# The attention output product on float16 parts for 24 of its 32 steps, and a new count of filler units around the heads

## The chip, the cores and the metric

The kernel runs on one core of a Trainium2 chip, in one launch. The metric is the device time of that core in microseconds. Before the change three runs took 1767.74, 1769.35 and 1769.62 us; their median, 1769.35 us, is the time before. The kernel's output must be the reference's in float32.

## The reference

A transformer of two layers with 256 tokens, 256 context tokens and 2048 model features, in float32. Layer 0 mixes by a Fourier transform, layer 1 by attention with 64 query heads and 8 key/value heads of 64 features, with a window, a context and a sink. Both end in an output product from 4096 branch features back to 2048. What bears on this case, cut:

```python
def _attend_with_sink(q, k, v, sink, mask=None):
    s = jnp.einsum('bqhgd,bkhd->bhgqk', q, k).astype(jnp.float32) * (ATTN_HEAD_DIM ** -0.5)
    ...
    p = jax.nn.softmax(jnp.concatenate([s, sk], axis=-1), axis=-1)[..., :-1]
    return jnp.einsum('bhgqk,bkhd->bqhgd', p.astype(v.dtype), v)

# _attention_branch
    y = jnp.moveaxis(o, 0, 1).reshape(b, n, D_BRANCH) * jax.nn.silu(z)

# reference, for each layer i
        h = _rmsnorm(x, norm_g[i]) * (1 + scale) + shift
        ...
        x = x + gate * (y @ w_out[i])
    return _rmsnorm(x, final_g)
```

With 256 tokens and 4096 branch features, y @ w_out[1] is a product of 256 x 4096 by 4096 x 2048: 32 steps of 128 branch features ("k" below), two blocks of 128 tokens ("tb") and four blocks of 512 columns.

## The kernel before, in words

**Numbers in two parts.** A float32 product is made of three matmuls on a high and a low part of each operand: high by high, high by low, low by high (`mm3`, lines 145 to 147). There are two kinds of parts. Float32r parts come from `split` (lines 66 and 67): ScalarE casts the high part, VectorE (in some places GpSimd) subtracts it for the low part. Float16 parts come from `split16` (lines 137 and 138): ScalarE writes the value times a power of two as float16, VectorE writes the rest; the power of two keeps the values in float16's range, and is found from a sum of squares of the whole operand. Before the change layer 0's products, the K/V product of layer 1 and the softmax weights use float16 parts; layer 1's q and z products and its output product use float32r parts.

**The stages around the change.**
- The Fourier output product (weights wo0, until about 1000 us) runs on float16 parts. Beside it, loads on GpSimd's queue bring tiles of 128 x 512 of the next weights (wkv), and ScalarE squares and sums them (line 827) for their scale.
- The K/V product: 8 weight groups (kg) of two steps each, one weight half of 128 x 1024 for each step, eight PSUM banks as its output. Then the evacuation (lines 1197 and 1198) and the making of v.
- Attention: 64 heads in a loop of 66 passes. Pass i has the scores of head i (lines 1422 and 1423), the softmax (1424 to 1430), the weights as float16 parts f (1439 on ScalarE, 1440 on VectorE), their transposition into ft, and the value product of head i − 2 (1457 and 1458). For heads 0 to 61 the transposition is a DMA on SP's queue (1442), for heads 62 and 63 sixteen transposes of TensorE (1449) and two copies (1450).
- Filler units. While one head's softmax runs, TensorE does pieces of other products: `filler()` is called twice in each pass and emits one unit. A unit is a piece of a q or z product (lines 1386 and 1388 and the lines of `mm3`), or two steps of the output product's first 512 columns (weights wo1a, `o1_step`, twelve matmuls). There are 64 units of q, 64 of z and 12 of the output product, 140; ten come ahead of the first head. 130 remain for 132 calls, so the last pass has none.
- The output product's rest: the remaining four double steps of wo1a, then wo1b (16 groups of two steps, columns 512 to 1535, 12 matmuls a step) and wo1c (8 groups of four steps, the last 512 columns, 6 matmuls a step), all on float32r parts. y's parts are made by `y_split`: steps 0 to 15 in a ring of tiles named ys, 16 to 23 in tiles of the pool act, 24 to 31 in another ring named ys.
- The end: gate, residual (x2), final norm, store.

**What sets the order.** Each engine works through its own row of instructions in order, and waits on semaphores. The row is set when the program is built, by a scheduler that follows the order of the code and its own model of times; `tc.issue_after(x)` keeps an instruction behind x. DMAs wait in their queue's row in the same way: SP's row carries the weight loads ("raw") and the DMA transposes, GpSimd's the tiles that are only squared and some others. Tiles come from rings with a fixed number of buffers: a load into a ring waits for the tile that was in its buffer before.

## Time and profile before

| | |
|---|---|
| median of three runs | 1769.35 us (1767.74 to 1769.62) |
| profiled execution, whole time | 1769.55 us |
| its span on the core | 1767.8 us |
| mean granted TensorE clock | 0.997 |
| Fourier output product | until about 1000 us |
| K/V product, TensorE | 1002.4 to 1085 us |
| attention, first scores to last value product | about 1127 to 1609 us |
| rest of the output product | about 1609 to 1759 us |
| norm and store after the last matmul | about 9 us |

The profile is of one execution. A row of a timeline has the start of a group, its time, the engine, the line, the operation, output and inputs, the count, and in brackets the idle time ahead of it with what ended it. Matmuls overlap in the array, so the duration of one is longer than the distance to the next; how long it holds TensorE is seen from one start to the next. A float32r matmul is shown as f32. A table of windows gives the busy time of each engine in each stretch, the granted clock, the busy share of the DMA engines and the rate that they moved.

### The profile page before, as it was taken

What the parts mean: (1) busy time and instruction counts of PE and PEld (TensorE: products, weight loads), DVE (VectorE), ACT (ScalarE), POOL (GpSimd) and SP (SyncE); (2) the same over time, 40 slices, a digit from 0 to 9 for tenths busy, and PEclk for the clock granted to TensorE, in tenths of its full rate; (3) what the DMA queues carried; (4) which work ended last, traced back from release to release, by engine and by line L of the source; (5) the groups of instructions that cost most, each with busy time, mean ns of one, the idle gap of its engine ahead of it and who ended that gap; (6) DMA issues with size and microseconds to landing.
All of it is one profiled execution on the core that took longest, in us unless ns stands there. A gap on an engine that the chain in (4) does not pass through costs nothing. (4 is left out here: it accounts for less than half of the span.)

```text
span 1767.8 us, 26608 instructions
## 1 busy us (share of the span) xinstructions
PE 1732.2 (98%) x9517; PEld 1187.7 (67%) x9517; DVE 1406.6 (80%) x2454; ACT 1090.5 (62%) x2069; POOL 331.9 (19%) x440
## 2 busy tenths in 40 slices
PE   6999999999999999999999999999999999999997
PEld 4679999644444444446444746788888888887886
DVE  5779889797677786877797695899999989997455
ACT  5545556477777755465223554687888878895343
POOL 0002111212222214212101001302312230233010
PEclk9999999999999999999999999999999999999999
DMA  9998998778998969977996432588988898887543
GB/s 394 417 356 247 279 278 254 289 286 314 332 305 312 312 228 371 368 267 259 341 316 212 142 137 74 169 215 199 223 207 206 213 215 206 207 212 258 190 167 143
DMA packets 229077, 447.29 MB, mean 253 GB/s; under 512 B 155888, under 2 KB 156288, under 8 KB 202064
## 3 DMA queue, kind: packets, MB, share of 16 engines
q1 hardware_dynamic: 182784, 331.93, 58.3%
q0 software_dynamic: 42016, 106.70, 19.4%
q10 hardware_dynamic: 4144, 6.95, 1.2%
q8 instruction: 75, 1.23, 0.3%
q14 instruction: 58, 0.48, 0.1%
HBM read 400.43 MB, written 12.59 MB: 234 GB/s over the span
## 5 line engine op out<-in xcount | busy, mean ns | idle before, releaser
L67 DVE TENSOR_TENSOR wl<-raw,wh 128x1024 fp32r<-128x1024 f32 x197 | 262.5, 1338 | 108.0 <-ACT wh L66 80.3
L66 ACT CAST wh<-raw 128x1024 fp32r<-128x1024 f32 x197 | 205.5, 1044 | 138.1 <-PE ps L146 97.0
L146 PE MATMUL ps<-act,wf 128*128 128x512 f16 x512 | 194.0, 379 | 0.0
L147 PE MATMUL ps<-act,wf 128*128 128x512 f16 x512 | 191.1, 379 | 0.0
L145 PE MATMUL ps<-act,wf 128*128 128x512 f16 x512 | 189.8, 379 | 0.6 <-ACT wf L137 0.2
L1386 PE MATMUL ps<-h,wh 128*128 128x512 f32 x512 | 185.0, 397 | 0.0
L145 PE MATMUL ps<-y,wf 128*128 128x512 f16 x448 | 169.8, 379 | 0.8 <-ACT wf L137 0.8
L147 PEld LDWEIGHTS <-wf 128*128 128x128 f16 x960 | 93.8, 98 | 114.0 <-DVE wf L138 0.9
L146 PE MATMUL ps<-y,wf 128*128 128x512 f16 x448 | 169.8, 379 | 0.0
L145 PEld LDWEIGHTS <-wf 128*128 128x128 f16 x960 | 93.7, 98 | 113.3 <-ACT wf L137 4.2
L147 PE MATMUL ps<-y,wf 128*128 128x512 f16 x448 | 167.4, 379 | 0.4 <-DVE wf L138 0.4
L146 PEld LDWEIGHTS <-wf 128*128 128x128 f16 x960 | 93.9, 98 | 109.0
L137 ACT ACTIVATE wf<-raw,nrm 128x1024 f16<-128x1024 f32 x56 | 63.4, 1145 | 137.1 <-DVE acc L792 68.5
L1388 PE MATMUL ps<-h,wl 128*128 128x256 f32 x512 | 138.6, 281 | 0.0
L138 DVE SCALAR_TENSOR_TENSOR wf<-raw,tn,wf 128x1024 f16<-128x1024 f32 x64 | 79.8, 1281 | 42.0 <-ACT wf L137 41.9
L1440 DVE SCALAR_TENSOR_TENSOR f<-p,sm,f 128x512 f16<-128x512 f32 x128 | 105.8, 847 | 9.0 <-ACT f L1439 8.7
L790 POOL DMA_DIRECT2D wa<-in_adw x64 | 34.0, 532 | 403.2 <-PE ps L147 149.7
L1427 ACT ACTIVATE p<-ps,mx 128x512 f32<-128x512 f32 x128 | 87.9, 689 | 35.0 <-DVE mx L1424 29.6
L1439 ACT ACTIVATE f<-p,sm 128x512 f16<-128x512 f32 x128 | 88.1, 717 | 34.3 <-DMA ft<-f 15.6
L1386 PEld LDWEIGHTS ps<-h,wh 128*128 128x128 f32 x512 | 96.4, 188 | 19.1
L827 ACT ACTIVATE act<-act 128x512 f32<-128x512 f32 x160 | 98.4, 616 | 6.0 <-DMA act<-in_wo 4.5
L146 PE MATMUL ps<-wl,h 128*128 128x512 f32 x256 | 101.3, 396 | 0.0
(414 smaller groups left out, 4672.8 us busy)
## 6 DMA issues: line engine op xcount, KB each, us to landing
raw<-in_wz SPq DMA_DIRECT2D x64, 1024.0 KB, 5.4
raw<-in_awp SPq DMA_DIRECT2D x32, 1024.0 KB, 12.7
zr<-in_adw SPq DMA_DIRECT2D x64, 512.0 KB, 6.8
wa<-in_adw POOLq DMA_DIRECT2D x64, 512.0 KB, 6.5
act<-in_wo POOLq DMA_DIRECT2D x128, 256.0 KB, 7.5
raw<-in_wo SPq DMA_DIRECT2D x32, 1024.0 KB, 7.7
raw<-in_wq SPq DMA_DIRECT2D x32, 1024.0 KB, 5.2
raw<-in_wu SPq DMA_DIRECT2D x32, 1016.0 KB, 6.5
```

Source lines behind the costliest of these rows:

```text
L66: last_cast[0] = S.copy(h, src).ins
L67: last_sub[0] = eng.tensor_tensor(l, src, h.bitcast(F32), op=ALU.subtract).ins
L138: last_sub[0] = V.scalar_tensor_tensor(w[:, 1], src, up, w[:, 0], op0=ALU.mult, op1=ALU.subtract).ins
L145: PE.matmul(o, wh, xh, start=start, stop=False)
L146: PE.matmul(o, wh, xl, start=False, stop=False)
L147: return PE.matmul(o, wl, xh, start=False, stop=stop).ins
L827: S.activation(t, t, AF.Square, accum_out=c)
L1386: PE.matmul(o[0], wh[:, q], hx1[k], start=k == 0, stop=k == KT - 1)
L1388: PE.matmul(o[0][:, 0:N], wl[:, q], hx1[k][:, 0:N], start=False, stop=False)
L1427: S.activation(pt[tb], so[tb], AF.Exp, bias=mx[:, tb : tb + 1], scale=-1.0, accum_out=sm[:, tb : tb + 1])
L1439: S.activation(f[:, 0:512], pt[tb], AF.Copy, scale=sm[:, tb : tb + 1])
L1440: V.scalar_tensor_tensor(f[:, 512:1024], pt[tb], sm[:, tb : tb + 1], f[:, 0:512], op0=ALU.mult, op1=ALU.subtract)
```

## The change

1. **Float16 parts.** For steps 0 to 23 of wo1b and wo1c the weights are split by `split16` with a scale uw, and y by the new `y_half` with a scale uy, one call for a pair of steps (twelve pairs). Steps 24 to 31 stay on float32r parts, with the weights multiplied by uw·uy (`w_scaled`) so that they sum into the same banks. The gate of those columns (`gbc[:, 512:]`) is multiplied by the inverse, dn1. Wo1a stays as it was.
2. **The scales.** uw comes from the sums of squares of 36 more weight halves (of wo1b's first twelve groups and wo1c's first six). Nine are loaded and squared as 128 x 512 tiles beside the Fourier output product, 27 as tiles of 128 x 1024 named pz, in a ring of four, loaded on GpSimd's queue and squared by ScalarE (line 1177 after) during the K/V product. uy comes from twelve squares of y in attention (`y_sums`). `out_scale`, in pass 62, makes both out of the sums by one reduction, three matmuls of one column and five tiny operations.
3. **The count of units.** Eleven units come ahead of the first head, fifteen of the output product lie in attention; with 143 units all 132 calls of `filler()` emit one. The last double step of wo1a comes behind the first two groups of wo1b.
4. **Head 61** is transposed by TensorE as heads 62 and 63 are.
5. The loads of x2 are spread: one column block at the start, the others at groups 3, 5 and 7 of wo1b.

The diff, cut to its core:

```diff
+    wst = [a["wkv"][i] for i in range(8)] + [a["wo1b"][i] for i in range(12)] + [a["wo1c"][i] for i in range(6)]
-    scans1 = iter(range(16))
+    scans1 = iter(range(52))
...
-                nc.gpsimd.dma_start(t, a["wkv"][j // 2][:, c : c + 512])
+                nc.gpsimd.dma_start(t, wst[j // 2][:, c : c + 512])
...
+        w_rate = {10: 1, 11: 1, 14: 2, 15: 2, 16: 2, 17: 1, 18: 1, 20: 1, 22: 2, 24: 3, 26: 3, 27: 3, 28: 3}
...
-            scan_loads1({10: 1, 11: 1, 14: 2, 15: 2, 16: 2, 26: 2, 27: 2}.get(i, 1 - i % 2) if 10 <= i < 28 and i not in (12, 13) else 0)
+            scan_loads1(w_rate.get(i, 0))
...
+            def sums2(act_only):
+                for n in range(len(pend)):
+                    t, c = pend.pop(0)
+                    if n < 2 or act_only:
+                        S.activation(t, t, AF.Square, accum_out=c)
+                    else:
+                        V.tensor_tensor_reduce(t, t, t, 1.0, 0.0, ALU.mult, ALU.add, c)
+
+            def loads2(n):
+                for j in [next(scans1) for _ in range(n)]:
+                    t = kvp.tile([P, 1024], F32, tag="pz", name="pz", bufs=4)
+                    nc.gpsimd.dma_start(t, wst[j // 2][:, j % 2 * 1024 : j % 2 * 1024 + 1024])
+                    pend.append((t, scn[:, j - 25 : j - 24]))
...
-                    w = [split16(wr, i, upk) if kg or i else w0 for i in range(2)]
+                    w = []
+                    for i in range(2):
+                        w.append(split16(wr, i, upk) if kg or i else w0)
+                        with tc.issue_after(last_cast[0]), tc.issue_after(ends[min(kg * 4 + i * 2 + 1, 15)][0]):
+                            if kg * 2 + i < 12:
+                                sums2(kg < 3)
+                        with tc.issue_after(pow_end[0]):
+                            loads2((3, 3, 3, 2, 2, 2, 2, 2, 2, 2, 2, 1, 1, 0, 0, 0)[kg * 2 + i])
...
+            sums2(True)
+            V.tensor_reduce(yq[:, 17:18], scn, axis=AX.X, op=ALU.add)
...
+            def y_sums(n, i):
+                while ynext[0] < min(n, len(ypairs)) and ypairs[ynext[0]] <= i - 2:
+                    j = ynext[0]
+                    ynext[0] += 1
+                    S.activation(act(), y1[j], AF.Square, accum_out=yq[:, j : j + 1])
...
+            def y_half(j):
+                t = h1p.tile([P, 1024], F16, tag="h1", name="yf", bufs=16)
+                S.activation(t[:, 0:512], y1[j], AF.Copy, scale=uy)
+                V.scalar_tensor_tensor(t[:, 512:1024], y1[j], uy, t[:, 0:512], op0=ALU.mult, op1=ALU.subtract)
+                for i in range(2):
+                    yf[j * 2 + i] = t[:, i * N : i * N + N], t[:, 512 + i * N : 512 + i * N + N]
...
+            def w_scaled(t, i):
+                h, l = (wsp.tile([P, 1024], F32R, tag="ws", name=n_) for n_ in ("wh", "wl"))
+                src = t[:, i * 1024 : (i + 1) * 1024]
+                last_cast[0] = S.activation(h, src, AF.Copy, scale=ub).ins
+                last_sub[0] = V.scalar_tensor_tensor(l, src, ub, h.bitcast(F32), op0=ALU.mult, op1=ALU.subtract).ins
+                return h, l
...
-                for k in range(12):
+                for k in range(15):
                     yield "o", k, 0, None
...
-                    if i < 62:
+                    if i < 61:
                         f = at.tile([P, 1024], F16, tag="f", name="f", bufs=3)
...
-            first = 10
+            first = 11
...
+                y_sums(12, i if i < 60 else 99)
+                if i == 62:
+                    out_scale()
                 if i < 64:
                     pts[i] = stage_s(i)
-                if i - 2 >= 62:
+                if i - 2 >= 61:
                     stage_t(*pts[i - 2])
...
+            with tc.issue_after(f_last[0]), tc.issue_after(f_last[1]):
+                for j in range(3):
+                    y_half(j)
...
             for kg in range(16):
-                w = ws_split(raw(a["wo1b"][kg]))
+                if kg == 2:
+                    first_rest()
+                t = raw(a["wo1b"][kg])
+                with tc.issue_after(f_last[0]), tc.issue_after(f_last[1]):
+                    w = [split16(t, i, uw) if kg < 12 else w_scaled(t, i) for i in range(2)]
+                if kg + 3 < 12:
+                    with tc.issue_after(last_cast[0]), tc.issue_after(last_sub[0]):
+                        y_half(kg + 3)
+                if kg in (3, 5, 7):
+                    x2_load(kg // 2)
...
-                    w = [(h[:, q], l[:, q]) for h, l in ws_split(t) for q in (slice(0, 512), slice(512, 1024))]
+                    w = [(h[:, q], l[:, q]) for h, l in (split16(t, i, uw) for i in range(2)) for q in (slice(0, 512), slice(512, 1024))]
```

What this does to the engines' rows, at three places. In these rows ps is a PSUM bank, wh and wl a weight's parts, f a head's softmax weights, ft their transposed copy, v the values, hz the normed input of the K/V product.

TensorE at the last head, before: the end of head 63's sixteen transposes (line 1449) and the start of its value product (1457).

```order
L1449 LDWEIGHTS f
L1449 MATMUL ps<-ident_16387,f 128x128
L1457 LDWEIGHTS v
L1457 MATMUL ps<-ft,v 128x256
L1458 LDWEIGHTS v
L1458 MATMUL ps<-ft,v 128x256
```

After: of the fifteen matmuls that now stand between the transposes (line 1516) and the value product (1524), the last eight.

```order
L146 MATMUL ps<-wl,act 128x512
L147 MATMUL ps<-wh,act 128x512
L145 MATMUL ps<-wh,act 128x512
L146 MATMUL ps<-wl,act 128x512
L147 MATMUL ps<-wh,act 128x512
L145 MATMUL ps<-wh,act 128x512
L146 MATMUL ps<-wl,act 128x512
L147 MATMUL ps<-wh,act 128x512
L1524 LDWEIGHTS v
L1524 MATMUL ps<-ft,v 128x256
```

The value product of the last head followed its transposes at once, and now has output-product matmuls ahead of it; ahead of the value products of heads 61 and 62 stand 24 each.

ScalarE in the first half of the K/V product, before: the normed input (line 1154) and the high parts of the weights (137) in turn.

```order
L1154 ACTIVATE hz<-ht,adab 128x256 x2
L137 ACTIVATE wf<-raw,adab 128x1024 x2
L1154 ACTIVATE hz<-ht,adab 128x256 x4
L137 ACTIVATE wf<-raw,adab 128x1024 x2
L1154 ACTIVATE hz<-ht,adab 128x256 x4
```

After:

```order
L1158 ACTIVATE hz<-ht,adab 128x256 x4
L1177 ACTIVATE pz,scn<-pz 128x1024 x2
L137 ACTIVATE wf<-raw,adab 128x1024 x2
L1177 ACTIVATE pz,scn<-pz 128x1024
L1158 ACTIVATE hz<-ht,adab 128x256 x4
L1177 ACTIVATE pz,scn<-pz 128x1024
L137 ACTIVATE wf<-raw,adab 128x1024 x2
```

The squares of the newly loaded tiles stand between them, 27 in all; the last three stand ahead of two weight casts and of the evacuation.

SP's queue in the loop over the heads, before: one weight load (line 50) and the DMA transposes (1442) of about one head in turn.

```order
L50 DMA raw<-in_wz 128x2048
L1442 DMA_TRANSPOSE ft<-f 128x8x128 x3
L50 DMA raw<-in_wz 128x2048
L1442 DMA_TRANSPOSE ft<-f 128x8x128 x2
L50 DMA raw<-in_wq 128x2048
L1442 DMA_TRANSPOSE ft<-f 128x8x128 x2
```

After:

```order
L50 DMA raw<-in_wq 128x2048
L1509 DMA_TRANSPOSE ft<-f 128x8x128 x2
L50 DMA raw<-in_wq 128x2048 x2
L1509 DMA_TRANSPOSE ft<-f 128x8x128 x2
L50 DMA raw<-in_wz 128x2048
L1509 DMA_TRANSPOSE ft<-f 128x8x128 x2
```

Once in eight heads two loads stand ahead of a pair of transposes, and once two pairs follow each other.

More of the change, by code (lines that the diff above doesn't have):

```diff
@@ L1243, in y_split @@
             def y_split(k):
[L1244 to L1247 removed]
+                t = h1p.tile([P, 512], F32R, tag="h1", name="ys", bufs=16) if k < 28 else act(F32R) if k < 30 else fin[0].tile([P, 512], F32R, tag="ys", name="ys", bufs=2)
                 split(t[:, 0:N], t[:, N : 2 * N], y1[k // 2][:, (k % 2) * N : (k % 2 + 1) * N], GP if k < 24 else V)
@@ L1251, in o1_step @@
+            def w_scaled(t, i):
[4 more added lines that the diff above has]
+                return h, l
             def o1_step(k, os_, wh, wl):
-                while len(yh) <= min(k + 4, NB - 1) and (len(yh) < 24 or fin):
+                while len(yh) <= min(k + 4, NB - 1) and (len(yh) < 30 or fin):
@@ L1510, in tile_dit, with x2_load @@
             nc.gpsimd.dma_start(gbc, gated.broadcast_to([P, D]))
-            x2 = []
-            for tb in range(2):
-                x2.append([act() for _ in range(4)])
-                for c in range(4):
+            x2 = [[], []]
+            def x2_load(c):
+                for tb in range(2):
+                    x2[tb].append(act())
                     nc.gpsimd.dma_start(x2[tb][c], x1d[tb, :, c * 512 : (c + 1) * 512])
+            x2_load(0)
             fg = fp.tile([P, D], F32, name="fg")
@@ L1554, in step @@
             def step(k, tb, wh, wl, q=slice(0, 512), first=0, last=NB - 1):
-                mm3(o[tb][:, q], yh[k][:, tb * P : (tb + 1) * P], yh[k][:, N + tb * P : N + (tb + 1) * P], wh[:, q], wl[:, q], k == first, k == last)
+                mm3(o[tb][:, q], *(t[:, tb * P : (tb + 1) * P] for t in y_parts(k)), wh[:, q], wl[:, q], k == first, k == last)
             def finish(tb):
@@ L1595, in tile_dit @@
                             for j in range(2):
-                                h, l = act(F32R), act(F32R)
-                                split(h, l, t[:, (i * 2 + j) * 512 : (i * 2 + j + 1) * 512])
+                                if kg == 6:
+                                    h, l = act(F32R), act(F32R)
+                                    src = t[:, j * 512 : j * 512 + 512]
+                                    S.activation(h, src, AF.Copy, scale=ub)
+                                    V.scalar_tensor_tensor(l, src, ub, h.bitcast(F32), op0=ALU.mult, op1=ALU.subtract)
+                                    w.append((h, l))
+                                    continue
+                                src = t[:, (i * 2 + j) * 512 : (i * 2 + j + 1) * 512]
+                                hl = actp.tile([P, 1024], F16, tag="act", name="wf")
+                                h, l = hl[:, 0:512], hl[:, 512:1024]
+                                S.activation(h, src, AF.Copy, scale=uw)
+                                V.scalar_tensor_tensor(l, src, uw, h, op0=ALU.mult, op1=ALU.subtract)
                                 w.append((h, l))
                         else:
-                            h, l = half_split(t, i)
+                            h, l = w_scaled(t, i)
                             w += [(h[:, q], l[:, q]) for q in (slice(0, 512), slice(512, 1024))]
```

48 lines of the change are left out of this document (33 added, 15 removed).

## The prediction

> **What bounds the kernel now.** I read the page's totals first, then a table of four stretches, then TensorE's timeline where it pauses.
>
> ```profile
> span 1767.8 us, 26608 instructions
> PE 1732.2 (98%) x9517; PEld 1187.7 (67%) x9517; DVE 1406.6 (80%) x2454; ACT 1090.5 (62%) x2069; POOL 331.9 (19%) x440
> core 0: us, PE busy (x) PEld busy (x) DVE busy (x) ACT busy (x) POOL busy (x), PEclk, DMA share, GB/s
> 830.00:985.00 155.00, 154.57 (x714) 75.02 (x712) 118.08 (x192) 49.79 (x77) 23.99 (x45) 1.00 0.79 284
> 1005.00:1081.00 76.00, 76.00 (x354) 34.48 (x353) 56.34 (x109) 36.96 (x62) 0.00 (x0) 1.00 0.39 130
> 1200.00:1500.00 300.00, 298.69 (x1635) 248.00 (x1635) 280.06 (x517) 242.85 (x476) 69.97 (x50) 1.00 0.86 209
> 1613.00:1758.00 145.00, 145.00 (x636) 117.74 (x635) 79.58 (x82) 58.70 (x70) 12.61 (x8) 1.00 0.52 179
> ```
>
> TensorE is busy 98% of the span, and in the four stretches that the change touches (end of the Fourier output product, the K/V product, attention, the attention output product) it is busy 155 of 155, 76 of 76, 299 of 300 and 145 of 145 us at full clock. So the time moves by what TensorE is given to do, and by waits put into or taken out of its row. The other engines matter only if they come to make it wait.
>
> How long one 512-column matmul holds TensorE is read from start to start, not from the duration of one.
>
> ```profile
> 599.98 0.38 PE L145 MATMUL ps<-act,wf 128*128 128x512 f16 x1
> 605.16 0.38 PE L145 MATMUL ps<-act,wf 128*128 128x512 f16 x1
> ...
> 1641.64 1.10 PE L145 MATMUL ps<-wh,ys 128*128 128x512 f32 x4
> 1644.44 1.10 PE L145 MATMUL ps<-wh,ys 128*128 128x512 f32 x4
> ...
> 1672.37 1.07 PE L145 MATMUL ps<-wh,act 128*128 128x512 f32 x4
> 1675.09 1.07 PE L145 MATMUL ps<-wh,act 128*128 128x512 f32 x4
> ```
>
> Float16 parts, in the Fourier output product: 24 matmuls between the first two rows, (605.16 − 599.98)/24 = 215.8 ns. Float32 parts, in wo1b: 12 between each of the other pairs, 2.80/12 = 233.3 ns where y lies in a "ys" tile and 2.72/12 = 226.7 where it lies in an "act" tile (steps 16 to 23).
>
> **Part 1: the number format.** wo1b issues 12 matmuls for each of the 32 steps, wo1c 6. Steps 0 to 23 go to float16: 24 x 12 = 288 and 24 x 6 = 144, 432 in all. Steps 0 to 15 save 16 x 18 x 17.5 ns = 5.0 us, steps 16 to 23 save 8 x 18 x 10.9 = 1.6. I take 6.5; had all been at 226.7 it were 4.7, at 233.3 7.6. The preparing of parts lies beside this: in the last stretch DVE is busy 80 and ACT 59 of 145 us, and one kind of split takes the place of another:
>
> ```profile
> L67 DVE TENSOR_TENSOR wl<-raw,wh 128x1024 fp32r<-128x1024 f32 x197 | 262.5, 1338 | 108.0 <-ACT wh L66 80.3 <-PE ps L147 18.4 <-issue 7.8
> L66 ACT CAST wh<-raw 128x1024 fp32r<-128x1024 f32 x197 | 205.5, 1044 | 138.1 <-PE ps L146 97.0 <-PE ps L147 33.3 <-DMA raw<-in_wo1c 3.3
> L138 DVE SCALAR_TENSOR_TENSOR wf<-raw,tn,wf 128x1024 f16<-128x1024 f32 x64 | 79.8, 1281 | 42.0 <-ACT wf L137 41.9
> L137 ACT ACTIVATE wf<-raw,tn 128x1024 f16<-128x1024 f32 x64 | 70.0, 1139 | 5.2 <-DVE tn L118 3.9 <-DVE tn L119 1.0 <-DMA raw<-in_wz 0.3
> L1440 DVE SCALAR_TENSOR_TENSOR f<-p,sm,f 128x512 f16<-128x512 f32 x128 | 105.8, 847 | 9.0 <-ACT f L1439 8.7
> L1439 ACT ACTIVATE f<-p,sm 128x512 f16<-128x512 f32 x128 | 88.1, 717 | 34.3 <-DMA ft<-f 15.6 <-issue 12.1 <-ACT th L1394 5.0
> L827 ACT ACTIVATE act<-act 128x512 f32<-128x512 f32 x160 | 98.4, 616 | 6.0 <-DMA act<-in_wo 4.5 <-DMA act<-in_wkv 1.6
> L827 ACT ACTIVATION_READ_ACCUMULATOR act<-act 128x1 f32 x160 | 30.0, 188 | 0.0
> ```
>
> One weight half costs ACT 1.14 for 1.04 and DVE 1.28 for 1.34. The twelve y pairs cost ACT 0.72 and DVE 0.85 each by the nearest rows (L1439, L1440, the same forms on half weights in attention). In wo1b a step group is 24 x 0.216 = 5.2 us of TensorE against 2 x 1.28 + 0.85 = 3.4 of DVE and 3.0 of ACT. Cost: nothing.
>
> [...]
>
> **Part 2: the end of attention.** TensorE's timeline with heads 61 to 63:
>
> ```profile
> 1593.82 0.40 PE L1423 MATMUL ps<-kkl,qb 128*128 128x512 f32 x1
> 1595.05 0.27 PE L1457 MATMUL ps<-ft,v 128*128 128x256 f16 x1 [0.83 <-DMA ft<-f]
> ...
> 1595.92 0.83 PE L1449 MATMUL ps<-ident,f 128*128 128x128 f16 x12
> 1596.56 0.48 PE L145 MATMUL ps<-wh,act 128*128 128x512 f32 x1
> ...
> 1604.78 0.40 PE L1449 MATMUL ps<-ident,f 128*128 128x128 f16 x4
> 1606.09 0.40 PE L1449 MATMUL ps<-ident,f 128*128 128x128 f16 x4 [0.91 <-DVE f L1440]
> 1608.15 0.28 PE L1457 MATMUL ps<-ft,v 128*128 128x256 f16 x1 [1.67 <-DVE ft L1450]
> ```
>
> Three pauses, start to start less the work between (0.23 for a matmul of 512 columns; twelve transposes took 0.64, 0.053 each): 1595.05 − 1594.05 = 1.0 for the DMA transposes of head 61, 1606.09 − 1605.0 = 1.1 for head 63's low part, 1608.15 − 1606.3 = 1.8 for its transposed copy. Sum 3.9. Afterwards 24, 24 and 15 output-product matmuls (5.6, 5.6 and 3.5 us at 0.233) stand between the transposes of heads 61, 62, 63 and the products that use them; before, 24 stood around head 62's, four between the halves of head 63's and none behind. From head 63's last score to its last transposes it was 12 us with the waits; it becomes 0.9 + 5.6 + 0.9 + 0.9 + 5.6 + 0.9 + 0.7 = 15.5. Head 61 no longer waits for DMA. Walking DVE's new row from head 63's scores with the mean durations above, the closest meeting is head 63's value product, with some 0.25 us in hand. I take all 3.9 as gone, and 0.3 for one new short wait (0 to 1.8, the longest of the three). Added: 16 transposes, 16 x 0.053 = 0.9 us, and three one-column matmuls for the scale, 0.1. The scale's five tiny DVE operations stand ahead of nothing that TensorE needs before wo1b, 15 us later. What gets late next is the first float16 weights of wo1b: both engines have those 15 us for them. The unit moved behind wo1b's second group, with its evacuation, holds two more of the eight banks for 10 us while wo1b uses four; the spread x loads go out on POOL, 13 of 145 us busy. Nothing for either.
>
> **Part 3: the sums of squares.** The scale needs 36 more weight halves read. Nine go into the 830–985 stretch as 18 squares of 0.62 + 0.19: 14.5 us on an ACT busy 50 of 155, and 18 x 0.26 = 4.7 MB, which lifts 284 GB/s to 314. 27 go into the K/V stretch:
>
> ```profile
> L645 ACT ACTIVATE pz<-pz x12: 1060/1063/1068, 147.9 to 285.4; 128x1024 f32<-128x1024 f32 x12
> wa<-in_adw POOLq DMA_DIRECT2D x64, 512.0 KB, 6.5
> GB/s 394 417 356 247 279 278 254 289 286 314 332 305 312 312 228 371 368 267 259 341 316 212 142 137 74 169 215 199 223 207 206 213 215 206 207 212 258 190 167 143
> 1080.30 1.05 ACT L66 CAST wh<-raw 128x1024 fp32r<-128x1024 f32 x1 [9.30 <-PE ps L147]
> 1081.55 0.59 ACT L1197 COPY act<-ps 128x512 f32<-128x512 f32 x1 [0.20 <-PE ps L147]
> ```
>
> Each is a load of 0.52 MB and, by L645, 1.06 + 0.19 us of ACT: 27 x 1.25 = 33.8 us, against 76.0 − 37.0 = 39 idle. The loads are 14.2 MB beside 76 x 130 GB/s = 9.9: 24.0 MB in 76 us, 316 GB/s; the slices of 44 us show up to 417 elsewhere, 142 and 137 here (972 to 1060). Through four buffers at 6.5 to landing and some 2.5 to square and reissue, 27 loads take 27/4 x 9 = 61 us; POOL, which issues them, is idle there (0.00 busy). ACT is in order: behind a late square wait the next K/V weight's high part and, last, the evacuation at 1081.55, for which TensorE's next products need the banks. Bounds: nothing if the loads keep 316, 3 us at 304 (24.0/304 = 79 us). I take 1.0. Twelve squares of y in attention (12 x 0.80 = 9.6 us) lie on an ACT idle 57 of 300.
>
> **Part 4: the eleventh unit and the denser loop.** TensorE's work is the same in another order. From a head's scores to its value product stand 18.7 us of its own work on average (17.8 before), so its waits should not grow. The largest is at the first head:
>
> ```profile
> 1136.94 0.40 PE L147 MATMUL ps<-wh,h 128*128 128x512 f32 x1
> 1139.36 0.27 PE L1457 MATMUL ps<-ft,v 128*128 128x256 f16 x1 [2.03 <-DMA ft<-f]
> ...
> 1140.15 0.42 PE L1458 MATMUL ps<-ft,v 128*128 128x256 f16 x1
> 1140.36 0.42 PE L1457 MATMUL ps<-ft,v 128*128 128x256 f16 x1
> ...
> 1143.11 0.40 PE L1386 MATMUL ps<-h,wh 128*128 128x512 f32 x1
> ```
>
> It costs 1139.36 − 1137.17 = 2.2 and then runs at half rate (0.21 a step where 0.11 is usual) until 1143.1: 3.75 us for work of 2.15, so 3.8 in all. Between the first scores and this product stand 9.1 us of TensorE's work in both orders; I leave it as it is. [...]
>
> **Sum.** Against the profiled execution (1769.55; the median of the runs is 1769.35): −6.5 − 3.9 + 0.9 + 0.1 + 0.3 + 1.0 = −8.1, 1761.4; from the median 1761.2, so 1761.
>
> **Rivals.**
> - A, the forecast: 1761, own range 1757 to 1764. Chance 0.53.
> - C: the three pauses come back elsewhere, because DVE is as far behind as before (0.25 us in hand is little): 1761 + 3.9 = 1765. 0.14.
> - D: float16 buys nothing, so the change doesn't do what it says: 1761 + 6.5 = 1767.5. Against it the pairs of rows; for it that these were taken in different stages. 0.05.
> - E: the eleventh unit also covers the first head's wait: 1761 − 3.8 = 1757. Against it, equal work in the order. 0.08.
> - B, slower: the K/V stage. If the loads run at 270 GB/s (slices 4 to 8 of the page show 247 to 289 under other loads) the last square ends 24.0/270 − 76 = 13 us late and TensorE waits for the evacuation: 1761 − 1 + 13 = 1773. It decides below about 300 GB/s, where it eats the gain at 1 us for each 4 GB/s. 0.12.
> - F: in attention SP's row now has two weight loads running ahead of a pair of transposes once in eight heads. If each makes a value product wait, 8 x 1.0 gives 1769; with the half rate each time, 8 x 3.8 gives 1791. Against it: the load takes 5 us to land and the product stands 18.7 behind. 0.08, half of it slower.
>
> Faster by over 0.2% (3.5 us, about what a measurement of this kernel can tell from no change): A, C, E, 0.75. Within: D and half of F, 0.09. Slower: B and half of F, 0.16. The range: 1755.5 (E with the full 7.6 of part 1) to 1771, which leaves out most of B and the worse half of F.
>
> **What would show it.** Right: float16 matmuls of wo1b 216 ns apart and about 6.5 us less from its first matmul to its last; no pause over 0.5 us at heads 61 to 63; TensorE whole through the K/V stage and no idle ahead of the first q product. Wrong: an idle of TensorE released by a square or by the evacuation behind it, waits on DVE's transposed copies as before, or value products that wait for DMA transposes in the middle of attention.

## The result: slower, 1778.4 against 1768.6 us

The changed kernel takes 1778.44 us (median of four runs, 1775.52 to 1779.30), the kernel before, with one run more, 1768.55 (1765.78 to 1769.62). The ratio is 1.0057, interval 1.0041 to 1.0072. The forecast was 1761 with a range to 1771, and 0.75 for faster. The profiled execution took 1775.52 us, the lowest of the four, with a span of 1773.5; against the profiled execution before, 1769.55, that is 6.0 more where 8.1 less was worked out.

The totals of the changed kernel, and the stretches that were shown of the kernel before (the last begins later, since attention ends later):

```profile
span 1773.5 us, 26843 instructions
...
PE 1730.2 (98%) x9539; PEld 1152.0 (65%) x9539; DVE 1435.0 (81%) x2475; ACT 1146.5 (65%) x2197; POOL 363.8 (21%) x485
```

```profile
830.00:985.00 155.00, 155.00 (x717) 75.50 (x716) 119.80 (x195) 61.30 (x113) 33.80 (x63) 1.00 0.89 315
1005.00:1081.00 76.00, 76.00 (x354) 34.45 (x352) 56.98 (x109) 63.98 (x116) 12.19 (x23) 1.00 0.88 323
1200.00:1500.00 300.00, 292.98 (x1583) 242.85 (x1583) 283.60 (x499) 241.30 (x486) 72.05 (x50) 0.99 0.83 202
1640.00:1758.00 118.00, 118.00 (x539) 64.15 (x537) 74.40 (x72) 58.52 (x67) 13.30 (x6) 1.00 0.51 177
```

The stretches with the new loads and squares are as whole as before: TensorE is busy 155 of 155 and 76 of 76 us, at 315 and 323 GB/s. The last stretch is whole too. What is new stands in attention: 293.0 of 300 us where it was 298.7, and a clock of 0.99.

What TensorE waited for, in total, times and longest. The kernel before, then the changed one:

```profile
PE ps L1457 <- DMA ft<-f: 4.2, 4, 2.0
PE ps L1457 <- DVE ft L1450: 1.7, 1, 1.7
...
PE ps L1449 <- DVE f L1440: 0.9, 1, 0.9
```

```profile
PE ps L1524 <- DMA ft<-f: 14.5, 9, 5.1
```

The waits on VectorE at the end of attention are gone from the list. The waits of value products for DMA transposes have grown from 4.2 to 14.5 us, which is the last of the prediction's own signs of being wrong. Apart from the first head's 1.4 us and four under 0.9 us, they are these, in the timeline of the changed kernel's TensorE:

```profile
1241.90 0.27 PE L1524 MATMUL ps<-ft,v 128*128 128x256 f16 x1 [2.02 <-DMA ft<-f]
...
1366.30 0.27 PE L1524 MATMUL ps<-ft,v 128*128 128x256 f16 x1 [1.44 <-DMA ft<-f]
...
1429.56 0.27 PE L1524 MATMUL ps<-ft,v 128*128 128x256 f16 x1 [2.15 <-DMA ft<-f]
...
1554.37 0.40 PE L1524 MATMUL ps<-ft,v 128*128 128x256 f16 x1 [5.14 <-DMA ft<-f]
```

They belong to heads 13, 29, 37 and 53. Heads have eight positions against the filler units (8 units of q and 8 of z make a period of 16 units, which is 8 passes), and these heads are all at position 5. SP's row around head 13, before and after (start, time from the start of the row's first issue to the end of its last, line, operation, count):

```profile
1226.87 0.33 SPq L50 DMA_DIRECT2D raw<-in_wq  x1
1230.50 2.92 SPq L1442 DMA_TRANSPOSE ft<-f  x2
1234.87 0.33 SPq L50 DMA_DIRECT2D raw<-in_wq  x1
```

```profile
1225.98 8.10 SPq L50 DMA_DIRECT2D raw<-in_wq  x2
1234.46 5.40 SPq L1509 DMA_TRANSPOSE ft<-f  x2
1239.99 0.49 SPq L50 DMA_DIRECT2D raw<-in_wz  x1
```

Before, a load went out 3.6 us ahead of the transposes and the next one behind them. Now the second of two loads goes out at 1233.75, as soon as VectorE is done with the tile that was in its buffer (at 1233.73), 0.7 us ahead of them, and the pair of transposes takes 5.4 us to issue where it took 2.9.

From the trace's records I worked out three parts of a head's way, as means over heads 8 to 55 at the same position: from the end of its scores to its last softmax weights f, from there to the issue of the second transpose, and from that to its landing.

| kernel, position | scores to f | f to issue | issue to landing | sum |
|---|---|---|---|---|
| before, 5 | 12.8 | 0.0 | 3.3 | 16.0 |
| after, 5 | 15.5 | 1.0 | 5.6 | 22.0 |
| before, 6 | 11.3 | 0.0 | 4.2 | 15.5 |
| after, 6 | 15.9 | 0.0 | 4.9 | 20.8 |
| before, 2 | 8.5 | 0.8 | 5.4 | 14.8 |
| after, 2 | 10.5 | 0.1 | 3.4 | 14.0 |

TensorE's own work from scores to value product, without its idle time, grew from 17.8 to 20.3 us at position 5, by 2.5; the parts' lateness grew by 6.0. Positions 1 to 4 of the changed kernel have 2 to 4 us in hand. The longest wait, at head 53, has a reason of its own besides: the parts land 22.8 us after the scores, much as at heads 13, 29 and 37, but 17.7 us of work stand ahead of its value product where the others have 20.8 to 21.0.

The records also show where the weight loads went. I call a load in flight at a transpose when it was issued ahead of it and was still more than 1.5 us from landing. At position 5 that held for none of twelve transposes before and for all twelve after; at positions 1 to 4 for 44 of 48 before and for 3 of 48 after. With a load in flight a transpose landed 5.2 us after its issue in the kernel before and 5.7 in the changed one (medians), without one 3.1 in both. So the shift took the loads away from heads whose weights f come early (8.5 to 9.1 us after the scores before the change) and put them on heads whose f come late (11.3 to 12.8 at positions 5, 6, 7 and 0).

### The profile page after: what moved, and what is told of

The parts are those of the page before. It is cut to its first block, busy times and chain, and to the rows that moved or that the text cites. A ratio compares the mean times of both kernels' runs of the same rounds, so it can differ in the third digit from the quotient of the medians.

```text
span 1773.5 us, 26843 instructions
## 1 busy us (share of the span) xinstructions
PE 1730.2 (98%) x9539; PEld 1152.0 (65%) x9539; DVE 1435.0 (81%) x2475; ACT 1146.5 (65%) x2197; POOL 363.8 (21%) x485
## 5 line engine op out<-in xcount | busy, mean ns | idle before, releaser
L67 DVE TENSOR_TENSOR wl<-raw,wh 128x1024 fp32r<-128x1024 f32 x152 | 203.4, 1339 | 33.1 <-ACT wh L66 22.5
L66 ACT CAST wh<-raw 128x1024 fp32r<-128x1024 f32 x152 | 158.0, 1040 | 48.8 <-PE ps L146 28.8
L1507 DVE SCALAR_TENSOR_TENSOR f<-p,sm,f 128x512 f16<-128x512 f32 x128 | 110.4, 886 | 10.9 <-ACT f L1506 10.5
L829 ACT ACTIVATE act<-act 128x512 f32<-128x512 f32 x178 | 109.4, 616 | 5.4 <-DMA act<-in_wo 4.4
## 6 DMA issues: line engine op xcount, KB each, us to landing
raw<-in_awp SPq DMA_DIRECT2D x32, 1024.0 KB, 12.8
```

The costliest lines, as they stand in the source:

```text
L66: last_cast[0] = S.copy(h, src).ins
L67: last_sub[0] = eng.tensor_tensor(l, src, h.bitcast(F32), op=ALU.subtract).ins
L829: S.activation(t, t, AF.Square, accum_out=c)
L1507: f_last[:] = fa, V.scalar_tensor_tensor(f[:, 512:1024], pt[tb], sm[:, tb : tb + 1], f[:, 0:512], op0=ALU.mult, op1=ALU.subtract).ins
```

## The experiments

Theory P: the eleventh unit shifts the units against the heads, and with it everything that the scheduler sets by them. Theory Y: the squares of y on ScalarE make the softmax weights late. Theory D: the heavier traffic of the new loads makes the transposes late. A ratio is to runs of the kernel before that were made at the same time. The diffs are cut, and are against the changed kernel, in run 2 against the kernel before; where ten units are named, run 1's edit is in it as well.

**1. Ten units instead of eleven.**

```diff
-                for k in range(15):
+                for k in range(14):
...
-            first = 11
+            first = 10
...
-                for k in range(30, NB, 2):
+                for k in range(28, NB, 2):
```

> The changed kernel, with ten units ahead of the first head instead of eleven and fourteen units of the output product in attention instead of fifteen (so that again every filler call emits one); float16 parts, squares, head 61 and the rest stay. Theory P (the place of the units: an eleventh unit shifts every later unit by one call against the heads, and at every eighth head the softmax weights come late on VectorE and ScalarE): the waits of 1 to 5 us at heads 13, 23, 29, 37, 48 and 53 go, the time is 1769 - 6.5 - 3.9 + 1.0 = about 1760, under 1764 in any case. Theory Y (the twelve squares of y on ScalarE delay the softmax weights): they are still there, so the waits stay and the time stays at 1774 to 1779. Theory D (the heavier DMA traffic of the new loads delays the transposes): the same as Y, no change from 1774 to 1779.

Measured: 1763.16 us, 0.9974 of before (0.9961 to 0.9986). TensorE's waits for transposes, from the list of its waits:

```profile
PE ps L1524 <- DMA ft<-f: 3.1, 3, 2.0
```

Y and D fall as the main cause: all squares and loads are in this kernel. The eleventh unit costs 15.3 us between the medians. The time is under P's bound of 1764 and 3 us above its sum.

**2. The kernel before with eleven units.**

```diff
-            first = 10
+            first = 11
```

> The kernel before, with eleven units ahead of the first head instead of ten, and nothing else: float32r parts everywhere, no squares of y, no new loads, the last three filler calls empty. Theory P: the waits at every eighth head come back here, 10 to 16 us in the loop, and with the last passes short of units by one more the time is 1778 to 1788. Theories Y and D: neither squares nor loads are in it, so it stays within 4 us of 1769.

Measured: 1787.69 us, 1.0106 (1.0091 to 1.0121). TensorE's waits for transposes in this kernel:

```profile
PE ps L1457 <- DMA ft<-f: 19.4, 12, 3.3
```

The time lies in P's range. So the loss needs nothing of the float16 parts, their squares or loads. At position 5 the parts land 22.3 us after the scores, as in the changed kernel.

**3. Float16 parts with the old counts.**

```diff
-                for k in range(15):
+                for k in range(12):
...
-            first = 11
+            first = 10
...
-                    if i < 61:
+                    if i < 62:
...
-                for k in range(30, NB, 2):
+                for k in range(24, NB, 2):
```

(`i == 61` and `i - 2 >= 61` likewise.)

> The changed kernel with the old count: ten units ahead, twelve of the output product in attention, head 61 transposed by DMA, four double steps of wo1a behind the second group of wo1b. What is left of the change is the float16 parts and all that their scales need. Theory P: no new waits in the loop; the 6.5 us of the number format show alone, and of the three pauses at the end the first (head 61 by DMA) stays: 1769 - 6.5 + 0.1 and between 0 and 3.9 off for the pauses, so 1759 to 1763. Theories Y and D: waits of about 12 us in the loop, so 1770 to 1776.

Measured: 1773.21 us, 1.0021 (1.0006 to 1.0036), a miss by 10 us. The ten runs spread from 1766.75 to 1779.39; the profiled one took 1767.1, and in it the loop is quiet and the end is not:

```profile
PE ps L1524 <- DMA ft<-f: 2.8, 3, 2.1
PE ps L145 <- ACT wh L66: 2.3, 1, 2.3
...
PE ps L146 <- DVE wl L67: 1.5, 2, 1.1
...
PE ps L1524 <- ACT ft L1517: 1.4, 2, 0.7
```

With the old count there are no product matmuls left for the last heads, while ScalarE and VectorE also make the float16 parts of y and of the first weights. My reading, which no run tests by itself, is that the format's gain does not show unless the new count leaves product matmuls for the end of attention. What the runs at 1773 spent more than the profiled one is not known.

**4. Twelve units.**

```diff
-            first = 11
+            first = 12
```

> The changed kernel with twelve units ahead of the first head (fifteen of the output product, so one of the 132 filler calls is empty). Theory P: a shift by two calls is a whole pass, so the units meet the heads as with ten, one pass earlier; from a head's scores to its value product TensorE then has 20.7 us of work on average in its row against 18.7, and 14.7 at the first head against 9.1, so the waits of the loop go and the first head's too: about 1757 to 1761. Theories Y and D: 1772 to 1779, perhaps less the first head's 1.6 us.

Measured: 1790.60 us, 1.0124 (1.0109 to 1.0139). All theories missed. From the list of TensorE's waits:

```profile
PE ps L1524 <- DMA ft<-f: 19.5, 20, 2.2
...
PE ps L1524 <- ACT ft L1517: 6.9, 1, 6.9
```

TensorE's longer row between scores and value product (20.7 us) bought nothing: the weights f came 15 to 17 us after the scores at five positions of eight. So it is not the oddness of the count. The place of the units decides, but the length of TensorE's row does not tell how.

**5. The loads held behind the transposes, eleven units.**

```diff
-                        nc.sync.dma_start_transpose(ft[:, :, tb, :], f)
+                        t_last[i] = nc.sync.dma_start_transpose(ft[:, :, tb, :], f).ins
...
-                    raws1[src] = raw(a["wq"][n, i // 2] if kind == "q" else a["wz1"][n])
+                    with tc.issue_after(t_last[turn[0] - 2]) if turn[0] - 2 in t_last else nullcontext(): raws1[src] = raw(a["wq"][n, i // 2] if kind == "q" else a["wz1"][n])
```

(turn[0] is the pass.)

> The changed kernel (eleven units) in which each weight load of the loop is held behind the DMA transposes of the head whose value product comes in the same pass; SP's row then has one load and one pair of transposes in turn, as before the change, and the scheduler sets VectorE's and ScalarE's rows anew around it. In the changed kernel, at every eighth head (5, 13, ...), the weights were ready 15.5 us after the scores, the second pair of parts was issued 1.0 us later behind a load and landed 5.6 us after that, 22 us in all against 20.9 us of TensorE's own work. Theory L (the loads directly ahead of the transposes): issue at once and landing in 3 to 4 us, 19 us in all, the waits of the loop go: 1760 to 1766. Theory F (the softmax weights come late on VectorE, whatever SP does): still 15 us and over to the weights, waits of 1 us and more stay at most of the eight places: 1770 to 1778.

Measured: 1815.51 us, 1.0282 (1.0245 to 1.0318). Transposes now land 3.1 to 3.6 us after issue at seven positions of eight, and TensorE waits for them 0.5 us in all; but the loads go out too late and the weights with them:

```profile
PE ps L145 <- ACT wh L66: 18.0, 6, 4.6
...
PE ps L1451 <- ACT wh L66: 8.8, 4, 4.3
PE ps L1453 <- DVE wl L67: 7.9, 8, 1.4
...
PE ps L1524 <- DMA ft<-f: 0.5, 2, 0.3
```

So the loads ahead did hold the transposes up (in the changed kernel the second of a pair lands 4.9 to 5.6 us after its issue at positions 5, 6, 7 and 0), and cannot simply be put behind them. Both theories' times missed. The scheduler also set VectorE's and ScalarE's rows anew, so this run does not separate the late weights f from the slow landing.

**6. The loads on GpSimd's queue, eleven units.**

```diff
-                    raws1[src] = raw(a["wq"][n, i // 2] if kind == "q" else a["wz1"][n])
+                    raws1[src] = raw(a["wq"][n, i // 2] if kind == "q" else a["wz1"][n], nc.gpsimd if pos[0] >= 13 else None)
```

> The changed kernel with the q and z weight loads of the loop on GpSimd's queue, so that SP's row in the loop holds transposes alone; the bytes moved are the same and the loads go out when their buffer is free, as before. Theory Q (SP's in-order row: a transpose waits there behind a load that waits for its buffer): issue at once, landing in 3 to 4 us, waits gone: 1760 to 1766. Theory B (the load's bytes, moved at the same time, slow the transposes, whichever queue they are on): issue at once, but landing in 5 to 6 us as now where a load goes out just ahead, waits of 0.5 to 3 us stay at heads 13, 21, ...: 1770 to 1777. If GpSimd's row is late with the loads, waits for weights appear, over 1777.

Measured: 1788.64 us, 1.0137 (1.0099 to 1.0174). The list of TensorE's waits has:

```profile
PE ps L1524 <- DMA ft<-f: 22.2, 14, 3.8
```

Alone in SP's row, the transposes still land 6.4 us after issue at position 5 and 9.6 at position 3, and 3.3 at positions 2 and 4. That speaks for B: it is the transfer in flight, not its place in SP's queue. The time is above B's range.

**7 and 8. The same hold with ten and with twelve units** (the edit of run 5 on the kernels of runs 1 and 4).

> Ten units ahead and fourteen of the output product (as in the first run), with the loads held behind the transposes as well. SP's row has one load and one pair in turn already there, so theories L and Q expect 1763 as without it, within 3 us; if it is VectorE's row that counts (theory F) and the scheduler sets it anew, the time can move either way by more than that.

> Twelve units ahead (1790.6 us as it was), with the loads held behind the transposes. There the softmax weights were ready 16 to 17 us after the scores at four of eight heads and the parts landed 4 to 6 us after issue, against 20.7 us of TensorE's work. Theory L: landing falls to 3 to 4 us, 20 us in all, most of the waits of 0.5 to 2 us go: 1764 to 1774. Theory F: 16 us and over stay, the waits stay in the main: 1780 to 1790.

Measured: 1781.57 us, 1.0084 (1.0063 to 1.0105), and 1803.20, 1.0201 (1.0184 to 1.0219). Landing fell to 3.1 to 3.3 us at all positions with ten, and to 3.1 to 3.8 at six positions with twelve, and both kernels became slower than runs 1 and 4, by 18 and 13 us. With ten, TensorE waits 3.5 us at a z product for ScalarE's high parts, and at q products 5.8 us for VectorE's low parts against 1.5 in run 1. Theory L's times failed in runs 5, 7 and 8; its landing held.

**9. A copy of 1 MB beside the transposes, ten units.**

```diff
+                    if i % 8 == 5 and tb:
+                        with tc.issue_after(fa): nc.scalar.dma_start(spare, a["wz1"][0])
                     if i < 61:
```

(spare is a tile in memory that nothing reads.)

> Ten units ahead as in the first run (1763.2 us), with a copy of 1 MB from memory to memory issued from ScalarE's queue just ahead of the second pair of transposes of heads 5, 13, ..., 61 (eight copies); TensorE's and SP's rows are nearly those of the first run. It puts back what the eleven-unit order has at these heads, a large transfer in flight with the transposes, without the later softmax weights. At these heads the parts landed 3.1 us after issue, with 0.5 to 0.8 us in hand. Theory B (bytes in flight slow the transposes): landing in 5 to 6 us there, a new wait of 1.5 to 2.5 us at up to eight heads, some followed by half rate: 1770 to 1785. If the lateness of the weights on VectorE is what counts: within 3 us of 1763.

Measured: 1783.79 us, 1.0080 (1.0063 to 1.0097), 20.6 above run 1. From the list of TensorE's waits:

```profile
PE ps L1527 <- DMA ft<-f: 17.8, 15, 3.2
...
PE ps L146 <- DVE wl L67: 2.6, 3, 1.0
```

SP's row at head 13, in run 1 and with the copy:

```profile
1231.60 2.62 SPq L1509 DMA_TRANSPOSE ft<-f  x2
```

```profile
1230.78 6.32 SPq L1512 DMA_TRANSPOSE ft<-f  x2
```

The weights f at position 5 are no later than in run 1 (14.1 against 14.3 us after the scores). The second transpose is issued 2.8 us behind them instead of 0.1, because the first one's issue holds SP's row for 4.4 us instead of 1.2; it lands 3.7 us after its issue instead of 3.1. So B's time came true, and its lateness too, but more at issue than in landing. The waits at heads 13, 21, 29, 37 and so on are there, and a part of them at the heads behind; transposes account for 14.7 of the 20.6 us. A transfer of 1 MB in flight at the transposes of one head in eight is enough for a loss of the size that was to be explained. It is a copy within memory, and not a weight load, so the size need not be the same.

**10 and 13. One square of y instead of twelve**, with ten and with eleven units; eleven squares are left out.

```diff
-                    S.activation(act(), y1[j], AF.Square, accum_out=yq[:, j : j + 1])
+                    if j == 0: S.activation(act(), y1[j], AF.Square, accum_out=yq[:, j : j + 1])
...
-                V.tensor_reduce(yq[:, 18:19], yq[:, 0:12], axis=AX.X, op=ALU.add)
+                V.tensor_scalar(yq[:, 18:19], yq[:, 0:1], 12.0, None, op0=ALU.mult)
```

> Ten units ahead as in the first run, with one square of y in attention instead of twelve; the sum is taken as twelve times the first, so the scale of y is less exact and eleven squares of 0.80 us are left out. Theory: they lie on ScalarE's idle time and cost nothing: within 2 us of 1763. Rival Y: they delay the weights of attention: 1755 to 1760.

> The changed kernel (eleven units, 1778 us) with one square of y in attention instead of twelve, the sum taken as twelve times the first; eleven squares are left out. With ten units this gave 2.7 us. Theory P with B (place of the units, loads in flight with the transposes): the waits at every eighth head stay, a gain of 1 to 4 us, 1774 to 1778. If the squares are what makes the weights late in the eleven-unit order too, the waits go: 1762 to 1768.

Measured: 1760.44 us, 0.9953 (0.9937 to 0.9970), and 1781.26, 1.0071 (1.0050 to 1.0091). With ten units the eleven squares cost 2.7 us between the medians, not nothing (run 1 and run 10 were made at different times, and their intervals overlap; run 14 repeats run 10): without them the weights f come 8.1 to 12.7 us after the scores, with them 9.6 to 14.3. With eleven units the time is 2.8 us above the changed kernel's and above the ranges of both theories; nothing is gained. In the list of its TensorE's waits those for the transposes stay:

```profile
PE ps L1524 <- DMA ft<-f: 19.6, 12, 5.0
```

**11. Head 0 transposed by TensorE, ten units.**

```diff
-                    if i < 61:
+                    if 0 < i < 61:
...
-                if i - 2 >= 61:
+                if i - 2 >= 61 or i == 2:
```

> Ten units ahead as in the first run, and head 0 transposed by TensorE like heads 61 to 63, instead of by DMA. The wait at the first value product was 2.15 us, ended by the DMA transposes, with half rate behind it, 3.8 us in all; the transposes add 0.9 us, and the copies (0.7 us on ScalarE and VectorE) take the place of 3 us of landing. Gain 0 to 3 us: 1760 to 1763, if the scheduler leaves the rest of the loop as it is.

Measured: 1772.08 us, 1.0021 (1.0011 to 1.0031). A miss: the wait of 2.0 us became another of 7.8, for the copy of the transposes, which the scheduler had put in ScalarE's row behind softmax weights of later heads, and which takes 1.0 us on ScalarE. In TensorE's timeline:

```profile
1148.76 0.37 PE L1524 MATMUL ps<-ft,v 128*128 128x256 f16 x1 [7.78 <-ACT ft L1517]
```

**12. Eight units.**

```diff
-                for k in range(15):
+                for k in range(12):
...
-            first = 11
+            first = 8
...
-                for k in range(30, NB, 2):
+                for k in range(24, NB, 2):
```

> The changed kernel with eight units ahead of the first head and twelve of the output product in attention (132 units for 132 calls), four double steps of wo1a behind wo1b's second group. In the built program SP's row has one load and one pair of transposes in turn, and 15.9 us of TensorE's work stand between the first scores and the first value product against 9.1. Theory P (the place of the units against the heads, as it shows in these rows): the first head's wait of 3.8 us goes and the loop has no regular waits: 1757 to 1763. If the number of units ahead matters only as the sum of work before the first head, or if the loop is limited elsewhere, it is no better than ten: 1763 or more.

Measured: 1770.43 us, 1.0011 (0.9998 to 1.0025). The first head's wait at its value product is gone and the loop has one wait of 2.4 us, much as P had it; but P's time missed by 7 us, since the two units fewer uncover the chain that makes the first q (rotation, transposes, parts) ahead of the first scores. In TensorE's timeline:

```profile
1115.25 0.66 PE L1370 MATMUL ps<-ident,act 128*128 128x128 f32 x2 [4.35 <-DVE act L1138]
1116.90 1.54 PE L1370 MATMUL ps<-ident,act 128*128 128x128 f32 x6 [0.99 <-DVE act L1138]
1119.78 0.79 PE L1489 MATMUL ps<-kkh,qa 128*128 128x512 f32 x1 [1.34 <-DVE qa L1375]
```

**14 and 15. Run 10 again, and without the 27 loads and squares of the K/V stage**, which are left out there.

```diff
-                            loads2((3, 3, 3, 2, 2, 2, 2, 2, 2, 2, 2, 1, 1, 0, 0, 0)[kg * 2 + i])
+                            loads2(0)
...
-            V.tensor_reduce(yq[:, 17:18], scn, axis=AX.X, op=ALU.add)
+            V.tensor_scalar(yq[:, 17:18], yq[:, 16:17], 3.0, None, op0=ALU.mult)
```

> The kernel of the tenth run again (ten units, one square of y; eleven squares are left out), for a firmer interval and against the run of this call: 1759 to 1763, 0.3 to 0.6% faster than before the change.

> The same, without the 27 loads and squares of weight halves in the K/V stage (the sum of squares of the weights is taken as three times that of the other tiles; 27 loads and squares are left out). Theory: that stage's loads and squares lie beside a busy TensorE and cost nothing: within 2 us of the run before in this call. Rival B of the prediction, what is left of it: they cost up to 3 us.

Measured: 1760.22 us, 0.9952 (0.9937 to 0.9968), and 1761.81, 0.9959 (0.9945 to 0.9973). The loads and squares of the K/V stage cost nothing that can be seen: without them the time is 1.6 us higher. Ten units with one square of y is the fastest version that was run, 0.48% below the kernel before, with the scale of y taken from one pair of twelve.

## Why the prediction was wrong, point by point

- **Part 1, the number format: right in the rate.** In the changed kernel's wo1b 24 float16 matmuls take 1685.02 − 1679.84 = 5.18 us, 215.8 ns each, as in the Fourier product; rival D is out. The whole of wo1b and wo1c was not timed against the kernel before. The first and the 25th in TensorE's timeline:

```profile
1679.84 0.38 PE L145 MATMUL ps<-wf,yf 128*128 128x512 f16 x1
...
1685.02 0.38 PE L145 MATMUL ps<-wf,yf 128*128 128x512 f16 x1
```

- **Part 2, the end of attention: right in the changed kernel.** No idle stands ahead of the value products of heads 61 to 63 in these rows; the sixteen transposes take 0.9 us:

```profile
1621.60 0.28 PE L1524 MATMUL ps<-ft,v 128*128 128x256 f16 x1
...
1622.49 1.06 PE L1516 MATMUL ps<-ident,f 128*128 128x128 f16 x16
...
1629.04 0.28 PE L1524 MATMUL ps<-ft,v 128*128 128x256 f16 x1
...
1634.05 0.28 PE L1524 MATMUL ps<-ft,v 128*128 128x256 f16 x1
```

- **Part 3, the sums of squares: right in the K/V stage**, with 323 GB/s measured for 316 worked out, ScalarE busy 64 of 76 us and a term of 1.0 that came to nothing. **Wrong in size for the squares of y**: "idle 57 of 300" took idle time of ScalarE as free, but the squares stand in its row ahead of softmax weights. They cost 2.7 us with ten units. Rival B is out: no wait of TensorE for a square or for the evacuation is in the list.
- **Part 4 is the step that failed**: "From a head's scores to its value product stand 18.7 us of its own work on average (17.8 before), so its waits should not grow." The two averages hold in the traces (18.7 and 17.7); the step from them to "no more waits" does not. The average hid that heads differ by position. And only one side was moved: the time until the parts are there was taken as it was, though the same shift sets VectorE's, ScalarE's and SP's rows anew. At position 5 it grew by 6.0 us against 2.5 of work to cover it: 2.7 for later weights f, 1.0 at issue, 2.3 in landing. TensorE's waits for transposes rose from 4.2 to 14.5 us.
- **Rival F** had the place (two loads ahead of a pair of transposes, once in eight heads), and its two times, 1769 and 1791, lie on either side of the 1778 measured; it was given 0.08. Its counter-argument, "the load takes 5 us to land and the product stands 18.7 behind", missed that the load goes out only when its buffer is free, at head 13 0.7 us ahead of the transposes; at position 5 the second one lands 5.6 us after its issue, where it was 3.3.
- **Rival E** came true in part: the first head's wait fell to 1.4 us in the profile, without half rate behind it (granted clock 1.00 from 1136 to 1144, where it was 0.79). That hid some of the loss. Run 1 has the full wait of 2.0 us there and no half rate either (no value-product matmul of line 1524 takes over 0.283 us; in the kernel before it is up to 0.418), so the missing half rate is not the eleventh unit's doing.
- **The sum.** Between the profiled executions of the changed kernel and of run 1, TensorE's wait for transposes differs by 14.5 − 3.1 = 11.4 us. Behind the waits of 2.0, 2.1 and 5.1 us the changed kernel ran at half rate for a while (granted clock 0.50 from 1243.2 to 1246.4, 1430.9 to 1434.1 and 1553.8 to 1557.0), 4.0 us in all by the distances between its matmuls; run 1 did not (its granted clock from 1200 to 1500 is 1.00). Run 1 has 3.1 us more in the rest of the list of waits. Together that is 12.3 of the 12.5 us between the two times.
- **What was left without the eleventh unit.** Run 1 is 5.3 us faster than the kernel before, and the forecast's 8.1 less 2.7 for the squares of y is 5.4. That the totals agree so closely is partly luck: run 1's list lacks the pauses at the end of attention, as forecast, but has 3.2 us of other short waits that are new, and the half rate behind the first head's wait, 1.5 us in the kernel before, is missing in it.
- **A slip.** The range's lower bound, 1755.5, comes to about 1756 by its own terms (1757 − 1.1). Nothing hangs on it.

What stays open: how the loss splits between later weights f and slower issue and landing, since the edits of runs 5, 7 and 8 also made the scheduler move VectorE's and ScalarE's rows. An estimate from the table's means: with the changed kernel's work of 20.3 us ahead of the product, either alone would have been covered on average (12.8 + 1.0 + 5.6 = 19.4 with the old f, 15.5 + 0.0 + 3.3 = 18.8 with the old issue and landing), and both together, 22.0, were not. Run 9 shows that in the ten-unit order, with 18.3 us of work ahead, the transfer in flight alone can do it. Why the scheduler's rows put f later with eleven units was not followed up.

## What to carry to other kernels

Here a count that shifted the fillers against the loop moved the other engines' rows too: at position 5 the softmax weights f came 2.7 us later, the second transpose was issued 1.0 us later behind them and took 2.3 us longer to land. So compare, by position in the period and not by an average, the work that covers a transfer with the time until the transfer is there, and look for a load that is released straight ahead of a small transfer that the next step waits for. In this kernel one unit more ahead of the loop cost 15 us, more than the change of format was worth (6.5, an estimate from the distances between matmuls in the kernel before). Ask also what stands late in a row behind new work: ScalarE was idle 57 of 300 us, and eleven squares of y in its row ahead of softmax weights still cost 2.7 us with ten units.

## What the runs showed of the hardware

- DMA transposes of 128 x 1024 float16, heads 8 to 55, medians from issue to landing: without a weight load of 1 MB in flight 3.1 us in the kernel before, the changed kernel and run 1; with one 5.2, 5.7 and 5.6. With the loads on another queue (run 6) it was 3.2 and 6.5. The issue itself also took longer with a transfer in flight: the pair of head 13 took 2.6 us in run 1 and 6.3 beside the copy of run 9.
- Behind a wait of 2.0 us the changed kernel ran at half rate from 1243.2 to 1246.4 us, at a granted clock of 0.50: 0.43 us for a 512-column matmul that takes 0.23. It did so behind waits of 2.1 and 5.1 us too; the three cost 4.0 us beyond their idle time. Behind waits of 1.4 us, at the first head and at 1366.3, the granted clock stayed at 1.00. The length of the wait alone did not decide: at the first head a wait of 2.0 us was followed by half rate in the kernel before (granted clock 0.51 from 1139.7 to 1143.1) and not in run 1 (no value-product matmul of line 1524 over 0.283 us). In the timeline of the changed kernel's TensorE, behind the wait at 1241.90:

```profile
1243.36 0.63 PE L1489 MATMUL ps<-kkh,qa 128*128 128x512 f32 x1
1243.79 0.63 PE L1490 MATMUL ps<-kkl,qa 128*128 128x512 f32 x1
```
